# Order of the 512- and 256-column products in each projection chunk, and the pooling product in two sums

## The chip, the cores and the metric

The kernel runs on one core of a Trainium2 chip. The metric is device microseconds of one execution. The kernel before took 885.79 us, the median of three runs (885.66 to 886.0). A run with the profiler on gives the trace from which everything below is read.

## The reference

A two-layer encoder trunk over 256 tokens of 1024 channels in float32. Each layer has a token mixer and a gated MLP, both after an RMSNorm and with a residual:

```
u, q, k, v, g_pool, g_attn = split(norm(h) @ w_in)
pooled   = centred_mean(u[group], window) - u[group]       # 4 groups of 256 channels
pool_out = einsum('bsgc,gcd->bsgd', pooled, w_pool) * pool_scale
attn_out = dilated attention over q, k, v                   # 12 heads in 3 groups
merged   = sigmoid(g_pool) * (pool_out @ w_a) + sigmoid(g_attn) * (attn_out @ w_b)
h = h + merged @ w_o
h = h + (gelu(conv3(a)) * g) @ w_down,   a, g = split(norm(h) @ w_up)
```

After the second layer comes a last RMSNorm.

## The kernel before

**Products in parts.** TensorE multiplies operands of type fp32r. To keep the accuracy, every float32 operand is split in two: a high part (the value cast to fp32r, by ScalarE) and a low part (the value minus the high part, by VectorE). A product is then the sum of three: high by high, low by high, high by low. For a weight this is `wh` and `wl` (lines 177 and 178); for the activations the high and low parts of one channel block lie side by side in the tile `x2` (shape: 8 channel blocks, 2 parts, 256 tokens), so that `x2[:, k]` is 512 columns (both parts) and `x2[:, k, 0]` the 256 columns of the high part.

**A chunk.** `proj` (line 485) makes 128 output channels for all 256 tokens. For each of the 8 blocks of input channels, `two_sums` (line 478) issues two products into one PSUM tile of 512 columns: `wh(k)` over the 512 columns of `x2[:, k]` (line 482), and `wl(k)` over the 256 columns of `x2[:, k, 0]` into the right half of the tile (line 483). The two alternate, so a chunk is eight pairs of a 512-column and a 256-column product. The left half then holds high by high, the right half both mixed sums; ScalarE copies the right half out and VectorE adds the left (`add_up`, lines 503 and 504, or their scaled forms at 970 and 971).

**Where chunks stand.** A layer has 96 chunks: 8 for the pooling input (line 806), 24 for queries and keys (line 954), 8 for the product with `w_a` (line 979), 16 for the gates (line 989) and 40 for the up projection (lines 1072, 1081, 1082). In two layers that is 192. The product with `w_b` (line 1008) calls `two_sums` too, with 4 blocks, in 8 half chunks a layer. Everything else on TensorE (values, scores, residual products at lines 508 to 510, transposes) does not go through it. In the residual products, runs of 512-column products follow one another, and at the end runs of 256-column ones; each has a weight load of its own, as every product here has.

**The pooling branch.** For each of four groups, VectorE forms the window sums and `pd`, and the split of `pd` is kept in two tiles, `plh` for the high and `pll` for the low parts (lines 795, 796, 830 to 834). They take the buffers tagged `ybig` and `xn`. Later `pool_out` (line 835) multiplies them by `w_pool` with `chunk_mm` (line 471): per 128 output channels two blocks of three 256-column products, all into one sum of 256 columns. ScalarE scales this into the high part of `po2` (line 848), VectorE forms the low part (line 849). `pool_out` is a generator: one step of it, two such sums, is placed ahead of each of the four chunks of the second pair of heads (lines 952 to 954).

**Buffers and order.** PSUM has four buffers of 512 columns with the tag `mm`; chunk, gate and pooling sums take them in turn, and a buffer is free once its reader on VectorE is done. Weights come through three raw buffers, loaded by the queue on SyncE, and five split buffers for `wh` and `wl` each; `W.get` has the split of the next three pieces made ahead. The order of the instructions on each engine is fixed when the program is built.

Of the kernel before, what the change touches and what calls it, by code (L numbers as in the profile page):

```python
# [10 lines left out]
F32 = mybir.dt.float32  # L11
F32R = mybir.dt.float32r
AF = mybir.ActivationFunctionType
ALU = mybir.AluOpType
AX = mybir.AxisListType

P = 128
D = 1024
S = 256
DEPTH = 2  # L20
KD = D // P
# [183 lines left out]
def encoder(ctx, tc, x, w_in, w_pool, pool_scale, w_a, w_b, w_o, norm1, norm2, w_up, conv_w,  # L205
            conv_b, w_down, rel_bias, norm_f, onehot, edges, out):
    nc = tc.nc
    const = ctx.enter_context(tc.tile_pool(name="const", bufs=1))
    wpool = ctx.enter_context(tc.tile_pool(name="weights", bufs=1))
    big = ctx.enter_context(tc.tile_pool(name="big", bufs=1))  # L210
    sm = ctx.enter_context(tc.tile_pool(name="small", bufs=2))
    acc = ctx.enter_context(tc.tile_pool(name="acc", bufs=4, space=bass.MemoryType.PSUM))
    mmp = ctx.enter_context(tc.tile_pool(name="mmp", bufs=4, space=bass.MemoryType.PSUM))
# [21 lines left out]
    for l in range(DEPTH):  # L235
        for g in range(NG):
            c0 = C_V + g * 512
            slots = (("m2", 0, 2), ("m2", 1, 2), ("ybig",), ("at2",)) if g == 0 else ()
            for j in range(2):
                tag = "k1" if l == 0 and g == 1 and j == 0 else None  # L240
# [227 lines left out]
        nc.sync.dma_start(out=ov[:, t, 512:], in_=xn[:, 512:])  # L468
        yield

    def chunk_mm(ps, wh, wl, xh, xl, nk):

        for k in range(nk):
            nc.tensor.matmul(ps, wh(k), xh[:, k], start=(k == 0), stop=False)
            nc.tensor.matmul(ps, wh(k), xl[:, k], start=False, stop=False)
            nc.tensor.matmul(ps, wl(k), xh[:, k], start=False, stop=(k == nk - 1))

    def two_sums(ps, wh, wl, x2, nk):


        for k in range(nk):
            nc.tensor.matmul(ps, wh(k), x2[:, k], start=(k == 0), stop=False)  # L482
            nc.tensor.matmul(ps[:, 1], wl(k), x2[:, k, 0], start=False, stop=(k == nk - 1))  # L483

    def proj(x2):

        i, (wh, wl) = W.get()
        ps = mmp.tile([P, 2, S], F32, tag="mm", name="proj_ps")
        two_sums(ps, lambda k: wh[:, k, :], lambda k: wl[:, k, :], x2, KD)
        W.free(i)  # L490
        return ps[:, 0], ps[:, 1]

    def halves(a):

        return a.rearrange("p (t m) -> p t m", t=2)

    def in_order(a):

        return a.rearrange("p (m t) -> p t m", t=2)

    def add_up(out, sums):

        nc.scalar.copy(out=out, in_=sums[1])
        nc.vector.tensor_add(out=out, in0=sums[0], in1=out)  # L504
# [65 lines left out]
    def v_tile():  # L570
        return acc.tile([P, 512], F32, tag="acc", name="v_ps")
# [11 lines left out]
    def two_parts(tag, name):  # L583


        return big.tile([P, KD, 2, 2, P], F32R, tag=tag, name=name)
# [161 lines left out]
    for l in range(DEPTH):  # L748
# [25 lines left out]
        else:  # L774
            for g in range(NG):
                held = begun[0] if g == 0 else [W.get() for _ in range(4)]
                for t in range(2):
                    if g + t == 0:
                        ps = begun[1]
                    else:  # L780
                        ps = v_tile()
# [10 lines left out]
        g2 = gain(norm2[l])  # L792


        plh = big.tile([P, KD, 2, P], F32R, tag="ybig", name="plh")
        pll = big.tile([P, KD, 2, P], F32R, tag="xn", name="pll")
        pooled = {}
        for gi in range(3, -1, -1):
            w = WINDOWS[gi]
            u = sm.tile([P, 2, S + 2 * PAD], F32, tag="u", name="u")  # L800
            nc.vector.memset(u[:, :, 0:PAD], 0.0)
            nc.vector.memset(u[:, :, PAD + S :], 0.0)
            for j in range(2):
                if l == 0:
                    next(bias, None)
                add_up(in_order(u[:, j, PAD : PAD + S]), [halves(a) for a in proj(x2)])
            cur, n = u, S + 2 * PAD
            sh = 1
            while sh < w:
                nxt = sm.tile([P, 2, S + 2 * PAD], F32, tag="us", name="us")  # L810
                n -= sh
                nc.vector.tensor_add(
                    out=nxt[:, :, 0:n], in0=cur[:, :, 0:n], in1=cur[:, :, sh : sh + n]
                )
                cur = nxt
                sh *= 2
            hw = w // 2
            o = PAD - hw
            e = edge[:, gi, 0:hw].unsqueeze(1).to_broadcast([P, 2, hw])
            nc.vector.tensor_mul(out=cur[:, :, o : o + hw], in0=cur[:, :, o : o + hw], in1=e)  # L820
            if hw > 1:
                e = edge[:, gi, hw : w - 1].unsqueeze(1).to_broadcast([P, 2, hw - 1])
                r = slice(o + S - hw + 1, o + S)
                nc.vector.tensor_mul(out=cur[:, :, r], in0=cur[:, :, r], in1=e)
            pd = sm.tile([P, 2, S], F32, tag="us", name="pd")
            nc.vector.scalar_tensor_tensor(
                out=pd, in0=cur[:, :, o : o + S], scalar=1.0 / w, in1=u[:, :, PAD : PAD + S],
                op0=ALU.mult, op1=ALU.subtract,
            )
            ph, pl = plh[:, 2 * gi : 2 * gi + 2], pll[:, 2 * gi : 2 * gi + 2]  # L830
            pd = pd.rearrange("p k (m t) -> p k t m", t=2)
            nc.scalar.copy(out=ph, in_=pd)
            nc.vector.tensor_sub(out=pl, in0=pd, in1=ph.bitcast(F32))
            pooled[gi] = (ph, pl)
        def pool_out(po2):
            for j in range(2):
                i, (wh, wl) = W.get()
                for gg in range(2):
                    ph, pl = pooled[2 * j + gg]
                    for oc in range(2):  # L840
                        ps = mmp.tile([P, 2, P], F32, tag="mm", name="pool_ps")
                        cc = slice(oc * P, (oc + 1) * P)
                        chunk_mm(
                            ps, lambda k: wh[:, 2 * gg + k, cc], lambda k: wl[:, 2 * gg + k, cc], ph, pl, 2
                        )
                        c = 4 * j + 2 * gg + oc
                        sc = hps[:, l, c : c + 1]
                        nc.scalar.activation(po2[:, c, 0], ps, AF.Copy, scale=sc)
                        nc.vector.scalar_tensor_tensor(
                            out=po2[:, c, 1], in0=ps, scalar=sc, in1=po2[:, c, 0].bitcast(F32),  # L850
                            op0=ALU.mult, op1=ALU.subtract,
                        )
                    if gg:
                        W.free(i)
                    yield
# [87 lines left out]
        for m, c in enumerate(PAIRS):  # L943
            if m == 1:
                po2 = two_parts("m2", "po2")
                pool_parts = pool_out(po2)
# [4 lines left out]
            for n in range(4):  # L951
# [4 lines left out]
                scale = HD**-0.5 if n < 2 else 1.0  # L956
                if hd < HPG:
# [3 lines left out]
                        out=lo[:, hd], in0=src, scalar=scale, in1=hi[:, hd].bitcast(F32),  # L961
                        op0=ALU.mult, op1=ALU.subtract,
                    )
                    nc.vector.scalar_tensor_tensor(
                        out=lo[:, hd], in0=rest, scalar=scale, in1=lo[:, hd].bitcast(F32),
                        op0=ALU.mult, op1=ALU.add,
                    )
                else:
# [3 lines left out]
                        out=o, in0=src, scalar=scale, in1=o, op0=ALU.mult, op1=ALU.add  # L972
# [20 lines left out]
        for c in range(KD):  # L993
            th = gate(c)
            nc.vector.scalar_tensor_tensor(
                out=pa[:, c, :], in0=th, scalar=1.0, in1=pa[:, c, :], op0=ALU.add, op1=ALU.mult
# [3 lines left out]
        for c4 in range(2):  # L1000
            ths = [gate(4 * c4 + j) for j in range(4)]
            for j2 in range(2):
                i, (wh, wl) = W.get()
                for j in range(2):
                    c = 4 * c4 + 2 * j2 + j
                    ps = mmp.tile([P, 2, S], F32, tag="mm", name="b_ps")
                    cc = slice(j * P, (j + 1) * P)
                    two_sums(ps, lambda k: wh[:, k, cc], lambda k: wl[:, k, cc], at2, 4)
                    m = sm.tile([P, S], F32, tag="u", name="m")
                    add_up(m, (ps[:, 0], ps[:, 1]))  # L1010
                    nc.vector.scalar_tensor_tensor(
                        out=m, in0=ths[2 * j2 + j], scalar=1.0, in1=m, op0=ALU.add, op1=ALU.mult
                    )
                    nc.vector.tensor_add(out=m, in0=m, in1=pa[:, c, :])
                    m = halves(m)
                    nc.scalar.copy(out=mh[:, c], in_=m)
                    nc.vector.tensor_sub(out=ml[:, c], in0=m, in1=mh[:, c].bitcast(F32))
                W.free(i)
# [43 lines left out]
        held, ps = entry  # L1062
        first = keep_entry(ps)
        ps = v_tile()
# [106 lines left out]
```

## Time and profile before

| | |
|---|---|
| median of three runs | 885.79 us |
| the profiled execution | 885.33 us |
| its span in the trace | 883.5 us |
| TensorE busy | 875.9 us |
| weight loads busy | 755.9 us |
| VectorE busy | 676.8 us |
| ScalarE busy | 520.2 us |
| granted TensorE clock, mean | 0.998 |
| chunk products, 512 columns | 1408 + 128 |
| chunk products, 256 columns | 1408 + 128 |
| half-chunk products (`w_b`), of each width | 64 |
| pooling products, 256 columns | 96 |

The duration that the profile gives for a product (398 ns on average for 512 columns) is the time from its start to its modelled end. Products overlap: the next one starts before the last one's end. What a product costs the stream is therefore the distance from its start to the next start, and this is read from the timeline, where starts are printed to 10 ns. Over a stretch of many products the first and the last start give the pace exactly enough.

### The profile page before, as it was taken

How to read it: one execution, taken by the hardware profiler on the slowest of the kernel's cores; microseconds unless marked ns; L12 is line 12 of the kernel's file. 1: busy time of each engine (PE TensorE's matmuls, PEld its weight loads, DVE VectorE, ACT ScalarE, POOL GpSimd, SP SyncE). 2: the span in 40 equal slices, each digit the busy share in tenths (PEclk: the TensorE clock that was granted, in tenths of full speed). 3: DMA queues.
4: the chain of work that ended last, by engine and by line, in shares of the span. 5: the costliest groups of instructions: out<-in, count | busy, mean ns of one | idle time of the engine just before them, and what ended most of it. 6: DMA issues, size and time to landing. Idle time of an engine off the chain costs nothing.

```text
span 883.5 us, 12773 instructions
## 1 busy us (share of the span) xinstructions
PE 875.9 (99%) x4849; PEld 755.9 (86%) x4849; DVE 676.8 (77%) x1151; ACT 520.2 (59%) x913; POOL 13.1 (1%) x40
## 2 busy tenths in 40 slices
PE   9999999999999999999999999999999999999997
PEld 7889889888888888888888898889888888888886
DVE  6988785767869977877855977766778698787784
ACT  7745554556647756666645564554566477666663
POOL 1000000000000000000000000000000000000000
PEclk9999999999999999999999999999999999999999
DMA  9669744455555475465736555444556447455541
GB/s 332 230 205 307 239 145 144 143 179 188 185 187 191 146 236 190 154 227 191 239 119 213 168 191 191 143 152 134 191 191 218 156 154 231 172 198 187 187 144 48
DMA packets 125790, 164.47 MB, mean 186 GB/s; under 512 B 2995, under 2 KB 106107, under 8 KB 125600
## 3 DMA queue, kind: packets, MB, share of 16 engines
q1 hardware_dynamic: 125712, 163.65, 55.7%
q8 instruction: 38, 0.62, 0.3%
q14 instruction: 24, 0.20, 0.1%
q10 hardware_dynamic: 16, 0.00, 0.0%
HBM read 162.57 MB, written 3.69 MB: 188 GB/s over the span
## 4 chain that ended last, share of the span: by engine, by line
PE 99%; ACT 0%; POOL 0%; DVE 0%; issue 0%; POOLq 0%; ACTq 0%
PE proj_ps L482 41%; PE proj_ps L483 20%; PE res_ps L508 6%; PE res_ps L510 6%; PE v_ps L578 6%; PE res_ps L509 6%; PE v_ps L740 2%; PE b_ps L482 2%; PE v_ps L653 1%; PE pt_ps L903 1%; PE b_ps L483 1%; PE o_ps L924 1%; PE s_ps L874 1%; PE s_ps L869 1%; PE o_ps L920 1%; PE xt_ps L450 1%
## 5 line engine op out<-in xcount | busy, mean ns | idle before, releaser
L482 PE MATMUL proj_ps<-x,wh 128*128 128x512 f32 x1408 | 498.5, 398 | 0.0
L178 DVE TENSOR_TENSOR wl<-raw,wh 128x1024 fp32r<-128x1024 f32 x274 | 334.4, 1223 | 123.5 <-ACT wh L177 121.3
L177 ACT CAST wh<-raw 128x1024 fp32r<-128x1024 f32 x274 | 286.6, 1051 | 189.4 <-PE proj_ps L482 146.2
L483 PE MATMUL proj_ps<-x,wl 128*128 128x256 f32 x1408 | 394.1, 280 | 0.0
L482 PEld LDWEIGHTS proj_ps<-x,wh 128*128 128x128 f32 x1408 | 264.5, 188 | 63.6 <-issue 0.7
L483 PEld LDWEIGHTS proj_ps<-x,wl 128*128 128x128 f32 x1408 | 265.6, 189 | 0.9 <-issue 0.2
L508 PE MATMUL res_ps<-wh,actq 128*128 128x512 f32 (+1 forms) x184 | 70.5, 383 | 0.0
L510 PE MATMUL res_ps<-wh,actk 128*128 128x512 f32 (+1 forms) x184 | 70.1, 381 | 0.0
L509 PE MATMUL res_ps<-wl,actq 128*128 128x512 f32 (+1 forms) x184 | 70.0, 380 | 0.0
L482 PE MATMUL proj_ps<-po,wh 128*128 128x512 f32 x128 | 46.2, 402 | 0.0
L510 PEld LDWEIGHTS res_ps<-wh,actk 128*128 128x128 f32 x184 | 34.6, 188 | 7.0
L508 PEld LDWEIGHTS res_ps<-wh,actq 128*128 128x128 f32 x184 | 34.6, 188 | 6.9
L509 PEld LDWEIGHTS res_ps<-wl,actq 128*128 128x128 f32 x184 | 34.6, 188 | 6.2
L483 PE MATMUL proj_ps<-po,wl 128*128 128x256 f32 x128 | 35.7, 279 | 0.0
L1084 ACT ACTIVATE y<-a,prm 128x256 f32<-128x256 f32 x36 | 21.6, 599 | 18.9 <-DVE a L504 18.8
L1101 ACT ACTIVATE y<-y 128x256 f32<-128x256 f32 x44 | 18.3, 416 | 21.3 <-DVE y L1098 21.3
L482 PEld LDWEIGHTS proj_ps<-po,wh 128*128 128x128 f32 x128 | 24.0, 188 | 5.0
L416 ACT ACTIVATE junk<-h 128x512 f32<-128x512 f32 (+1 forms) x20 | 10.9, 547 | 27.7 <-DVE h L414 27.7
L508 PE MATMUL res_ps<-wh,m 128*128 128x512 f32 (+1 forms) x72 | 26.5, 368 | 0.0
L510 PE MATMUL res_ps<-wh,m 128*128 128x512 f32 (+1 forms) x72 | 26.3, 366 | 0.0
L509 PE MATMUL res_ps<-wl,m 128*128 128x512 f32 (+1 forms) x72 | 26.3, 365 | 0.0
L578 PE MATMUL v_ps<-wh,x 128*128 128x512 f32 x80 | 25.7, 392 | 0.0
(208 smaller groups left out, 1129.6 us busy)
## 6 DMA issues: line engine op xcount, KB each, us to landing
raw<-in_w_in_dram SPq DMA_DIRECT2D x58, 1024.0 KB, 5.4
raw<-in_w_up_dram SPq DMA_DIRECT2D x44, 1024.0 KB, 5.1
raw<-in_w_down_dram SPq DMA_DIRECT2D x22, 1024.0 KB, 4.9
raw<-in_w_a_dram SPq DMA_DIRECT2D x8, 1024.0 KB, 4.9
raw<-in_w_o_dram SPq DMA_DIRECT2D x8, 1024.0 KB, 4.9
raw<-in_w_b_dram SPq DMA_DIRECT2D x4, 1024.0 KB
sk<-fd SPq DMA_DIRECT2D x1, 2560.0 KB
raw<-in_w_pool_dram SPq DMA_DIRECT2D x2, 1024.0 KB
```

Of the source, the lines that this page charges most:

```text
L177: lambda: nc.scalar.copy(out=h, in_=src),
L178: lambda: nc.vector.tensor_sub(out=l, in0=src, in1=h.bitcast(F32)),
L416: nc.scalar.activation(junk[:, 0 : cc.stop - cc.start], h[:, t, cc], AF.Square, scale=D**-0.5, accum_out=ss[:, n : n + 1],)
L482: nc.tensor.matmul(ps, wh(k), x2[:, k], start=(k == 0), stop=False)
L483: nc.tensor.matmul(ps[:, 1], wl(k), x2[:, k, 0], start=False, stop=(k == nk - 1))
L508: nc.tensor.matmul(ps, ah, wh, start=first, stop=False)
L509: nc.tensor.matmul(ps, ah, wl, start=False, stop=False)
L510: nc.tensor.matmul(ps, al, wh, start=False, stop=last)
L578: nc.tensor.matmul(ps, x2[:, 2 * n + j, part, t, :], w[:, j, :], start=(n + m == 0), stop=(n == 3 and m == 5),)
L740: nc.tensor.matmul(ps[t], a[:, k, t, :], w[:, j, :], start=(k + m == 0), stop=(k == KD - 1 and m == 2),)
L1084: nc.scalar.activation(y, a, AF.Identity, bias=b, scale=w1)
L1101: nc.scalar.activation(y2, y2, AF.Tanh, scale=c)
```

## The change

`two_sums` issues first all products of 512 columns of a chunk, then all of 256. The pooled values are kept with both parts side by side, groups 0 and 1 in the buffer `ybig`, groups 2 and 3 in `xn`, so that `pool_out` can call `two_sums` (two products of 512 columns and two of 256 in place of six of 256) on a PSUM tile of 512 columns. The sum is then put together in a small tile `po`, from the buffers tagged `u`, and split from there: four operations in place of two for each 128 channels. `chunk_mm` goes.

```diff
     def two_sums(ps, wh, wl, x2, nk):
         for k in range(nk):
             nc.tensor.matmul(ps, wh(k), x2[:, k], start=(k == 0), stop=False)
+        for k in range(nk):
             nc.tensor.matmul(ps[:, 1], wl(k), x2[:, k, 0], start=False, stop=(k == nk - 1))
...
-        plh = big.tile([P, KD, 2, P], F32R, tag="ybig", name="plh")
-        pll = big.tile([P, KD, 2, P], F32R, tag="xn", name="pll")
+        pl2 = [
+            big.tile([P, KD // 2, 2, 2, P], F32R, tag=tag, name="pl2") for tag in ("ybig", "xn")
+        ]
...
-            ph, pl = plh[:, 2 * gi : 2 * gi + 2], pll[:, 2 * gi : 2 * gi + 2]
+            both = pl2[gi // 2][:, gi % 2 * 2 : gi % 2 * 2 + 2]
+            ph, pl = both[:, :, 0], both[:, :, 1]
...
-                        ps = mmp.tile([P, 2, P], F32, tag="mm", name="pool_ps")
+                        ps = mmp.tile([P, 2, S], F32, tag="mm", name="pool_ps")
                         cc = slice(oc * P, (oc + 1) * P)
-                        chunk_mm(
-                            ps, lambda k: wh[:, 2 * gg + k, cc], lambda k: wl[:, 2 * gg + k, cc], ph, pl, 2
+                        two_sums(
+                            ps, lambda k: wh[:, 2 * gg + k, cc], lambda k: wl[:, 2 * gg + k, cc],
+                            pooled[2 * j + gg], 2,
                         )
                         c = 4 * j + 2 * gg + oc
                         sc = hps[:, l, c : c + 1]
-                        nc.scalar.activation(po2[:, c, 0], ps, AF.Copy, scale=sc)
+                        po = sm.tile([P, 2, P], F32, tag="u", name="po")
+                        nc.scalar.mul(out=po, in_=halves(ps[:, 1]), mul=sc)
                         nc.vector.scalar_tensor_tensor(
-                            out=po2[:, c, 1], in0=ps, scalar=sc, in1=po2[:, c, 0].bitcast(F32),
-                            op0=ALU.mult, op1=ALU.subtract,
+                            out=po, in0=halves(ps[:, 0]), scalar=sc, in1=po, op0=ALU.mult, op1=ALU.add
                         )
+                        nc.scalar.copy(out=po2[:, c, 0], in_=po)
+                        nc.vector.tensor_sub(out=po2[:, c, 1], in0=po, in1=po2[:, c, 0].bitcast(F32))
```

More of the change, by code (lines that the diff above doesn't have):

```diff
@@ L469, in store @@
         yield
[L471 to L476, printed above, removed]
     def two_sums(ps, wh, wl, x2, nk):
@@ L833, in encoder @@
             nc.vector.tensor_sub(out=pl, in0=pd, in1=ph.bitcast(F32))
-            pooled[gi] = (ph, pl)
+            pooled[gi] = both
         def pool_out(po2):
@@ L838, in pool_out @@
                 for gg in range(2):
-                    ph, pl = pooled[2 * j + gg]
                     for oc in range(2):
-                        ps = mmp.tile([P, 2, P], F32, tag="mm", name="pool_ps")
+                        ps = mmp.tile([P, 2, S], F32, tag="mm", name="pool_ps")
                         cc = slice(oc * P, (oc + 1) * P)
-                        chunk_mm(
-                            ps, lambda k: wh[:, 2 * gg + k, cc], lambda k: wl[:, 2 * gg + k, cc], ph, pl, 2
+                        two_sums(
+                            ps, lambda k: wh[:, 2 * gg + k, cc], lambda k: wl[:, 2 * gg + k, cc],
+                            pooled[2 * j + gg], 2,
                         )
```

## The prediction, made before the changed kernel ran

> **What bounds the kernel now.** I read the page first: span, busy shares, and the chain that ended last.
>
> ```profile
> span 883.5 us, 12773 instructions
> PE 875.9 (99%) x4849; PEld 755.9 (86%) x4849; DVE 676.8 (77%) x1151; ACT 520.2 (59%) x913; POOL 13.1 (1%) x40
> PE 99%; ACT 0%; POOL 0%; DVE 0%; issue 0%; POOLq 0%; ACTq 0%
> ```
>
> The chain of waits is TensorE from end to end. So the time is the sum of the distances between the starts of products, and only a step that alters these distances counts, or one that makes another engine late enough to stop TensorE. Products overlap, so their own durations are no costs here.
>
> Second, the timeline of TensorE, for the distances. A pair (512 columns, then 256) in the MLP stage, and in the gates stage, first and last start of a stretch of nothing but pairs:
>
> ```profile
> 393.52 0.40 PE L482 MATMUL proj_ps<-x,wh 128*128 128x512 f32 x1
> ...
> 404.12 0.40 PE L482 MATMUL proj_ps<-x,wh 128*128 128x512 f32 x1
> ```
>
> ```profile
> 180.88 0.39 PE L482 MATMUL proj_ps<-x,wh 128*128 128x512 f32 x1
> ...
> 194.75 0.39 PE L482 MATMUL proj_ps<-x,wh 128*128 128x512 f32 x1
> ```
>
> The first is 30 pairs in 10.60 us, 0.3533 a pair; the second 40 pairs in 13.87, 0.3468. The same two instructions thus cost 2% more in one stage than in the other, with the clock at full speed in both. A view of such stretches by window, with TensorE's busy time and the number of products of the chunk tile, tells how the kernel divides:
>
> ```profile
> core 0: us, PE busy (x), PEclk, DMA share, GB/s
> 55.66:77.96 22.30, 22.30 (x128) 1.00 0.86 255
> 92.19:111.98 19.79, 19.79 (x112) 1.00 0.64 213
> 309.21:320.50 11.29, 11.29 (x64) 1.00 0.83 274
> 477.72:511.63 33.91, 33.91 (x192) 1.00 0.58 187
> 612.50:640.20 27.70, 27.70 (x160) 1.00 0.55 184
> ```
>
> Half the count is pairs: 0.348, 0.353, 0.353, 0.353 and 0.346 a pair. The DMA share does not follow the pace (0.86 in a cheap stretch, 0.58 in a dear one), so it is not the loads. I take the 80 chunks of the MLP by the row at 309.21 as dear, with the 12 at 477.72 and the 7 at 92.19; the 32 of the gates by the row at 612.50 as cheap, with the 8 at 55.66; the rest, between heads, as half and half. That is about 70 to 30: a chunk of eight pairs takes 8 x 0.3533 = 2.827 or 8 x 0.3468 = 2.774, 2.81 us on average.
>
> **The order in a chunk: 192 chunks.** It removes and adds no product; it turns eight pairs into a run of eight 512s and a run of eight 256s. Each needs its own price. A long run of 512s, well under way:
>
> ```profile
> 21.14 0.39 PE L740 MATMUL v_ps<-wh,xul 128*128 128x512 f32 x1
> ...
> 32.02 0.39 PE L740 MATMUL v_ps<-wh,xul 128*128 128x512 f32 x1
> ```
>
> 48 products in 10.88 us, 0.227 each. That would be 1.82 for eight. But a run does not begin at this pace when 256s stood before it. Three places of the trace show a run of 512s that follows a 256, each with its first and its ninth start:
>
> ```profile
> 303.76 0.40 PE L508 MATMUL res_ps<-wh,actq 128*128 128x512 f32 x1
> ...
> 305.58 0.39 PE L510 MATMUL res_ps<-wh,actk 128*128 128x512 f32 x1
> ```
>
> ```profile
> 234.27 0.39 PE L508 MATMUL res_ps<-wh,m 128*128 128x512 f32 x1
> ...
> 236.11 0.39 PE L510 MATMUL res_ps<-wh,m 128*128 128x512 f32 x1
> ```
>
> ```profile
> 320.50 0.40 PE L508 MATMUL res_ps<-wh,actq 128*128 128x512 f32 x1
> ...
> 322.37 0.40 PE L510 MATMUL res_ps<-wh,actk 128*128 128x512 f32 x1
> ```
>
> Eight cost 1.82, 1.84 and 1.87. In the last one that is 0.234 each, the price of the steady run not reached within a chunk's length. None of the three follows a run of 256s, only pairs, so for the new chunk I take the middle between the ends, 1.85, and keep both.
>
> A run of 256s after a run of 512s, first and ninth start, and one after pairs, the twelve of a pooling step up to the next chunk:
>
> ```profile
> 253.34 0.28 PE L508 MATMUL res_ps<-wh,m 128*128 128x256 f32 x1
> ...
> 254.29 0.28 PE L510 MATMUL res_ps<-wh,m 128*128 128x256 f32 x1
> ```
>
> ```profile
> 82.22 0.28 PE L474 MATMUL pool_ps<-plh,wh 128*128 128x256 f32 x1
> ...
> 83.66 0.40 PE L482 MATMUL proj_ps<-x,wh 128*128 128x512 f32 x1
> ```
>
> Eight cost 0.95 in the first; twelve cost 1.44 in the second, eight of them 0.96. The new chunk is 1.85 + 0.955 = 2.805 us, with ends 1.82 + 0.95 = 2.77 and 1.87 + 0.96 = 2.83, against 2.81: 192 x -0.005 = -1.0 us, with ends -7.7 and +3.8. The gain of a steady run is about eaten by the change of width, which a chunk now makes twice and hardly recovers from.
>
> The Trainium skill says under "TensorE: Matmul & The Clock Gate", in "Step-by-step: what each phase is for", that the weight load has an SBUF read port of its own and takes nothing from a running product; and in "Back-to-back issue gap" that the gap is the columns over 2.4 GHz plus 2.5 ns. An estimate by that page is 216 and 109 ns, 2.60 us a chunk in any order, so no gain at all from this step. The trace has 2.77 to 2.83, and two prices for one pair, so it disagrees, and the sum above goes by the rows.
>
> **The half chunks of `w_b`: 16.** They stand among the gates, at the cheap pace: 4 x 0.3468 = 1.387. New: half of what eight cost above, 0.91 to 0.935 for four 512s and 0.475 to 0.48 for four 256s, 1.385 to 1.415; with 1.40, 16 x 0.013 = +0.2 us.
>
> **The pooling product: 8 steps.** A step was the twelve 256s just shown, 1.44 us. It becomes twice (two 512s, two 256s), as many of each as a half chunk, 1.385 to 1.415, with two more changes of width that no row prices; with 1.40, 8 x -0.04 = -0.3 us.
>
> **The pooling sum's extra operations: 16 casts, 16 subtractions.** Nearest rows and the stage in both layers:
>
> ```profile
> L1017 DVE TENSOR_TENSOR m<-m,m 128x256 fp32r<-128x256 f32 x16 | 6.4, 420 | 0.0
> L1016 ACT CAST m<-m 128x256 fp32r<-128x256 f32 x16 | 6.2, 405 | 3.5 <-DVE m L1014 3.5
> 78.00:92.20 14.20, 14.20 (x99) 13.08 (x98) 11.65 (x17) 9.97 (x18) 0.00 (x0) 1.00 0.97 322
> 511.00:526.00 15.00, 15.00 (x102) 13.78 (x101) 9.50 (x15) 8.62 (x16) 0.00 (x0) 1.00 0.76 255
> ```
>
> Per layer VectorE gets 8 x 0.42 = 3.4 us more, ScalarE 8 x 0.41 = 3.2. In layer 0 VectorE has 14.20 - 11.65 = 2.55 free, so it falls behind by up to 0.8; in layer 1 it has 5.5, ScalarE 4.2 and 6.4. What is late next is the release of a PSUM buffer. The tightest one I find: VectorE's reads of the first two pooling sums start at 81.35 and last 0.87, the second set of sums takes the first of these buffers at 82.94, and the next chunk the other at 83.66.
>
> ```profile
> 81.35 0.87 DVE L849 SCALAR_TENSOR_TENSOR po<-pool_ps,hps,po 128x256 fp32r<-128x256 f32 x2
> 82.94 0.28 PE L474 MATMUL pool_ps<-plh,wh 128*128 128x256 f32 x1
> ```
>
> The buffers are free at 81.8 and 82.2, 1.1 and 1.4 us ahead. In the built order both reads still stand ahead of the new subtractions, and later ones are behind by at most 0.8. I cost this at nothing; without that cover it is 0.8 us. The small tile `po` shares two buffers with the pooling input, so ScalarE's scaling of one sum waits for VectorE's subtraction two sums earlier; behind it stand casts of weights, which run up to three pieces ahead.
>
> **Moved, at no cost.** `wh` is now read for the last time eight 256s (0.95 us) before the chunk's end, and `wl` for the first time 1.85 us after its start:
>
> ```profile
> ACT wh L177 <- PE proj_ps L482: 146.2, 127, 2.3
> ```
>
> ScalarE waits 146 us in all for `wh` to be read out, off the chain; it may start earlier, `wl` has more time, and neither can stop TensorE more than before. The raw loads on SyncE's queue keep their order. The new buffers for the pooled values are each written later or freed no later than the old ones.
>
> Sum: -1.0 + 0.2 - 0.3 = -1.1 us on the profiled execution's 885.33 (a span of 883.5 and 1.8 around it), 884.2. The median of the runs, 885.79, stands 0.46 above it, so 884.7.
>
> **Rivals.** *The runs settle at once* (34%). The new chunk begins after eight 256s in step, not after pairs; if that is the better start, eight 512s cost 1.82 to 1.84 as at 303.76 and 234.27, a chunk 2.77 to 2.80. With 2.785: 192 x -0.025 = -4.8, on the median's 885.8, so 881.0; at the end 878.1. For it: two of the three places. Against: at 320.50 eight products were not enough to settle.
>
> *Every chunk pays the dear start* (20%). Each chunk is the case of 320.50, with 256s that cost 0.96: 2.83, 192 x 0.02 = +3.8, 889.6. It decides once the eight 512s take over 1.865. For it: that place stands in the MLP, where 80 of the 192 chunks are; against: the last 256s of a run lie 0.12 apart, as regular as anything in the trace, whereas 320.50 comes out of the uneven pairs.
>
> *VectorE becomes the bound in the pooling stage* (3%). If the 0.8 us reach TensorE in both layers, with the chunk as forecast, +1.6: 886.4; it turns slower only with part of the second rival.
>
> **How the numbers follow.** What a measurement of this kernel can tell from no change I take as 0.2%, 1.8 us. My forecast, the switch of width costs what the pairs' unevenness cost, has 43%, and its own range is 884.0 to 887.5. Faster is the first rival, 34%; slower the second and third, 23%. The range reaches into both, short of the lowest end: 879.5 to 889.6.
>
> **What would show it.** In the changed profile, starts of line 482 from the first to the ninth product of a chunk (1.85 forecast, 1.82 or less and 1.87 or more the rivals), then eight 256s in 0.95 to 0.96; the same length for all chunks, no longer two paces; TensorE's idle column still 0.0 in front of pooling products; a pooling step of 1.40. I am wrong if a chunk lies outside 2.80 to 2.815, or if TensorE waits for VectorE anywhere.

## The result, and the profile after

The changed kernel took 881.65 us, the median of five runs (881.34 to 882.08), beside 885.77 for the kernel before in the same comparison (five runs, 885.02 to 886.0). The ratio is 0.9957, with a 95% interval of 0.9946 to 0.9968: faster by 0.43%, about 4.1 us. The profiled execution took 882.08 us.

The page of the changed kernel, span, busy shares, and the chain that ended last by engine:

```profile
span 880.3 us, 12800 instructions
...
PE 872.4 (99%) x4817; PEld 757.5 (86%) x4817; DVE 682.5 (78%) x1167; ACT 525.6 (60%) x929; POOL 14.0 (2%) x40
...
PE 99%; ACT 0%; POOL 0%; DVE 0%; issue 0%; POOLq 0%; ACTq 0%
```

The chain is TensorE from end to end, as before, and VectorE and ScalarE have become 5.7 and 5.4 us busier. So the gain must lie in the distances between products. The timeline of TensorE gives the first chunk's first product and the last chunk's first product of a run, in the kernel before and then in the changed one:

```profile
41.88 0.48 PE L482 MATMUL proj_ps<-x,wh 128*128 128x512 f32 x1
...
852.22 0.40 PE L482 MATMUL proj_ps<-x,wh 128*128 128x512 f32 x1
```

```profile
42.37 0.48 PE L475 MATMUL proj_ps<-x,wh 128*128 128x512 f32 x1
...
848.73 0.40 PE L475 MATMUL proj_ps<-x,wh 128*128 128x512 f32 x1
```

From the one to the other it is 810.34 us before and 806.36 after, 3.98 less. The first chunk started 0.49 later in this execution, though nothing ahead of it was changed; over the kernels of this study that start lay between 41.7 and 42.4. This stretch, called the *inner time* below, is free of that.

Each product's distance to the next start, summed in the trace by the tile that it writes, divides the 3.98 (us):

```
                                   before    after   difference
chunks                            539.69   536.42     -3.27
half chunks of w_b                 22.19    22.45     +0.27
pooling sums                       11.47    11.15     -0.32
residual products                 143.03   142.60     -0.42
transposes in the attention         6.63     6.33     -0.30
all others                         87.33    87.40     +0.07
```

The stretches of chunks, by window, answer to those shown of before, with the same chunks in each:

```profile
core 0: us, PE busy (x), PEclk, DMA share, GB/s
56.11:78.56 22.45, 22.45 (x128) 1.00 0.85 258
92.52:112.07 19.55, 19.55 (x112) 1.00 0.68 216
309.26:320.41 11.15, 11.15 (x64) 1.00 0.66 217
476.51:510.00 33.49, 33.49 (x192) 1.00 0.59 198
610.13:638.03 27.90, 27.90 (x160) 1.00 0.52 173
```

The window of twelve chunks at 476.51 went from 33.91 to 33.49 us, while the last, with the gates, went from 27.70 to 27.90: the two paces of the kernel before have become one, which lies between them. A chunk, from its first 512 over its first 256 to the next chunk:

```profile
98.10 2.00 PE L475 MATMUL proj_ps<-x,wh 128*128 128x512 f32 x8
99.94 1.11 PE L477 MATMUL proj_ps<-x,wl 128*128 128x256 f32 x8
100.89 0.40 PE L475 MATMUL proj_ps<-x,wh 128*128 128x512 f32 x1
```

The eight 512s take 1.84 us and the eight 256s 0.95. Of the 192 chunks, 134 follow another chunk directly. All of these cost 2.793 to 2.795; before, they cost 2.773 to 2.831, 2.810 on average. A chunk that follows a run of 512s is another case:

```profile
269.85 1.98 PE L475 MATMUL proj_ps<-x,wh 128*128 128x512 f32 x8
271.66 1.12 PE L477 MATMUL proj_ps<-x,wl 128*128 128x256 f32 x8
272.62 0.38 PE L1056 MATMUL a_turn<-ident,a_rows 128*128 128x128 f32 x2
```

Here the 512s take 1.81 us, 0.227 each from the first: 2.77 for the chunk. There are 17 such chunks (14 behind residual products, 3 behind those of the values), and before they cost 2.810. The distances of single products (in ns, from the trace) show where the chunk pays:

```
before, gates:        231 112  233 117  231 113  232 118 ...
before, MLP:          241 120  236 113  233 117  241 120  236 113  233 117 ...
after, behind a 256:  233 236 229 232 231 227 226 227   113 119 120 120 120 120 120 120
after, behind a 512:  226 227 227 226 227 227 226 227   113 119 120 120 120 120 120 120
```

In the settled state a 512 is 227 and a 256 is 120 apart, eight of each 2.774 us. The pairs of the gates alternate at this sum; the pairs of the MLP repeat a pattern of three that costs 53 ns more a chunk; the new order pays 27 ns in the first five 512s and has 8 back in the first two 256s.

### The profile page after: what moved, and what is told of

Read it like the earlier page. It is cut to its first block, busy times and chain, and to the rows that moved or that the text cites. A ratio compares the mean times of both kernels' runs of the same rounds, so it can differ in the third digit from the quotient of the medians.

```text
span 880.3 us, 12800 instructions
## 1 busy us (share of the span) xinstructions
PE 872.4 (99%) x4817; PEld 757.5 (86%) x4817; DVE 682.5 (78%) x1167; ACT 525.6 (60%) x929; POOL 14.0 (2%) x40
## 4 chain that ended last, share of the span: by engine, by line
PE 99%; ACT 0%; POOL 0%; DVE 0%; issue 0%; POOLq 0%; ACTq 0%
PE proj_ps L475 40%; PE proj_ps L477 21%; PE res_ps L502 6%; PE v_ps L572 6%; PE res_ps L503 6%; PE res_ps L504 6%; PE v_ps L734 2%; PE b_ps L475 2%; PE v_ps L647 1%; PE b_ps L477 1%; PE pool_ps L475 1%; PE o_ps L922 1%; PE s_ps L872 1%; PE pt_ps L901 1%; PE s_ps L867 1%; PE o_ps L918 1%
## 5 line engine op out<-in xcount | busy, mean ns | idle before, releaser
L475 PE MATMUL proj_ps<-x,wh 128*128 128x512 f32 x1408 | 354.1, 393 | 0.0
L475 PEld LDWEIGHTS proj_ps<-x,wh 128*128 128x128 f32 x1408 | 254.1, 189 | 47.3 <-issue 0.5
L477 PEld LDWEIGHTS proj_ps<-x,wl 128*128 128x128 f32 x1408 | 192.0, 190 | 13.8
L477 PE MATMUL proj_ps<-x,wl 128*128 128x256 f32 x1408 | 196.3, 282 | 0.0
L475 PE MATMUL proj_ps<-po,wh 128*128 128x512 f32 x128 | 33.1, 400 | 0.0
L1083 DVE SCALAR_TENSOR_TENSOR y<-a,prm,y 128x255 f32<-128x255 f32 x36 | 17.3, 480 | 8.1 <-ACT y L1082 8.1
```

Of the source, the lines that this page charges most:

```text
L1083: nc.vector.scalar_tensor_tensor(out=y[:, 1:], in0=a[:, : S - 1], scalar=w0, in1=y[:, 1:], op0=ALU.mult, op1=ALU.add)
```

## The experiments

**One half of the change at a time.** First the order in `two_sums` alone, with the pooling branch as in the kernel before:

```diff
         for k in range(nk):
             nc.tensor.matmul(ps, wh(k), x2[:, k], start=(k == 0), stop=False)
+        for k in range(nk):
             nc.tensor.matmul(ps[:, 1], wl(k), x2[:, k, 0], start=False, stop=(k == nk - 1))
```

> The order of the products alone; the pooling branch as before the change. Theory A (the price of a product depends on the widths that stand before it, and the chunks gave the gain): chunks of 2.793 us as in the changed kernel, pooling steps of 1.44 as before, so 881.65 + 8 x 0.045 = 882.0 us. Rival B (the pooling branch gave most of it): 885 or more. Rival C (the later need of wl gave it, by ending waits that the profile does not show): 882.0 too, but then the second product of the first pair, not the run, is where a chunk got shorter.

Then the pooling branch alone: the changed kernel with this one line taken out again.

> The pooling branch in two sums, with its products and those of all chunks alternating as before the change. Theory A: a pooling step is four pairs of 0.347 to 0.353 us, 1.39 to 1.41 in place of 1.44, and nothing else: 885.77 - 8 x 0.04 = 885.4 us. Rival B: 882.5 or less.

Measured: the order alone 882.01 us (881.83 to 882.32), ratio 0.9956 [0.9943, 0.9968]; the pooling branch alone 884.95 (884.35 to 886.92), ratio 0.9997 [0.9988, 1.0006], that is, no change. The inner times are 806.73 and 810.01, so 3.61 and 0.33 less than before, and these add up to 3.94 of the 3.98. With the order alone the chunks cost 2.793 again; with the pooling branch alone they keep their two paces, 2.810 on average. The gain is that of the order. That `wl` is needed later, the other explanation set down for the order, is not what brings it: groups of two and pairs in the gates, both below, need `wl` earlier again, and their chunks cost 2.787 and 2.774, less than the 2.793 of eight and eight.

**Other lengths of the runs.** If the price comes from each change of width, shorter runs must cost more; if it comes from a pattern of distances that each order settles into, it need not. Groups of two, and of four:

```diff
+GROUP = 2
...
-        for k in range(nk):
-            nc.tensor.matmul(ps, wh(k), x2[:, k], start=(k == 0), stop=False)
-        for k in range(nk):
-            nc.tensor.matmul(ps[:, 1], wl(k), x2[:, k, 0], start=False, stop=(k == nk - 1))
+        for k0 in range(0, nk, GROUP):
+            for k in range(k0, min(k0 + GROUP, nk)):
+                nc.tensor.matmul(ps, wh(k), x2[:, k], start=(k == 0), stop=False)
+            for k in range(k0, min(k0 + GROUP, nk)):
+                nc.tensor.matmul(ps[:, 1], wl(k), x2[:, k, 0], start=False, stop=(k == nk - 1))
```

> The changed kernel, with each chunk in four groups of two 512s and two 256s. Theory A: as the pooling step of the changed kernel, which is such groups, 1.394 us for four products of each width, so 2.788 a chunk against 2.793: 881.65 - 192 x 0.005 - 16 x 0.009 = 880.5 us. Rival D (each change of width costs, the longer the run the better): four times the changes of the changed kernel, 884 us or more, nearer to the pairs than groups of four are.

> The changed kernel, with each chunk in two groups of four 512s and four 256s. Theory A: as two half chunks of w_b in the changed kernel, 1.401 + 1.406 = 2.807 us a chunk: 881.65 + 192 x 0.014 = 884.3 us, slower than groups of two. Rival D: between groups of two and the changed kernel, faster than groups of two.

Groups of two: 880.47 us (879.85 to 880.66), ratio 0.9936 [0.9924, 0.9948]. Groups of four: 884.54 (883.72 to 885.47), ratio 0.9986 [0.9978, 0.9995]. The timeline of groups of two, the first products of two chunks in a row, and the same for groups of four:

```profile
186.19 0.63 PE L477 MATMUL proj_ps<-x,wh 128*128 128x512 f32 x2
...
188.98 0.62 PE L477 MATMUL proj_ps<-x,wh 128*128 128x512 f32 x2
```

```profile
187.31 1.09 PE L477 MATMUL proj_ps<-x,wh 128*128 128x512 f32 x4
...
190.11 1.09 PE L477 MATMUL proj_ps<-x,wh 128*128 128x512 f32 x4
```

The chunk costs 2.787 us (distances 233 231 113 119, then 233 236 116 112) against 2.807. With eight changes of width groups of two are cheaper than the new kernel with two changes, and groups of four, with four changes, are dearer than both. The number of changes does not set the price.

**Pairs where pairs are cheap.** The gates and the half chunks of `w_b` have got dearer by the change, 2.774 to 2.793 and 1.387 to 1.4035. Here they alternate again, and all other chunks stay as in the changed kernel. The switch is set to 1 ahead of the gates and back ahead of the MLP:

```diff
+        if GROUPS[0] == 1:
+            for k in range(nk):
+                nc.tensor.matmul(ps, wh(k), x2[:, k], start=(k == 0), stop=False)
+                nc.tensor.matmul(ps[:, 1], wl(k), x2[:, k, 0], start=False, stop=(k == nk - 1))
+            return
```

> The changed kernel, but with alternating pairs in the 32 chunks of the gates and the 16 half chunks of w_b; runs everywhere else. Theory A (what stands before decides the pace of the pairs, and here 128-column products stand before, as they did before the change): pairs at 0.3468, a chunk 2.774 in place of 2.793 and a half chunk 1.387 in place of 1.4035: 881.65 - 32 x 0.019 - 16 x 0.0165 = 880.8 us. Rival E (the pace belongs to the stage or drifts, and nothing in the order fixes it): pairs at 0.353 as in most stages, 881.65 + 32 x 0.034 + 16 x 0.01 = 882.9 us.

Measured: 880.59 us (880.52 to 881.03), ratio 0.9944 [0.9931, 0.9958]. Ten gate chunks, first and last start:

```profile
180.91 0.39 PE L477 MATMUL proj_ps<-x,wh 128*128 128x512 f32 x1
...
208.65 0.39 PE L477 MATMUL proj_ps<-x,wh 128*128 128x512 f32 x1
```

That is 2.774 a chunk: the price by place adds up. The pairs are cheap here although chunks of runs, not of pairs, stand in the stages ahead; what stands directly ahead in both kernels are the 128-column products of the attention. This run alone doesn't tell the stage from what stands ahead, since the gates were cheap before too. The kernel with the pooling branch alone does, at one place: in the pooling stage of layer 0 the first two chunks behind a pooling step cost 2.773 there, where the step consists of pairs, and 2.832 in the kernel before, where it is a run of 256s.

**Runs of sixteen.** Two chunks at a time: the 512s of both, then the 256s of both, for 168 of the 192 chunks. It needs two weights split and two PSUM buffers at once.

```diff
+        for ps, (_, (wh, _)) in zip(sums, got):
+            for k in range(KD):
+                nc.tensor.matmul(ps, wh[:, k, :], x2[:, k], start=(k == 0), stop=False)
+        for ps, (_, (_, wl)) in zip(sums, got):
+            for k in range(KD):
+                nc.tensor.matmul(ps[:, 1], wl[:, k, :], x2[:, k, 0], start=False, stop=(k == KD - 1))
```

> The changed kernel, with two chunks at a time in 168 of the 192: sixteen 512s, then sixteen 256s. Theory A: the second eight 512s and the second eight 256s cost what a settled run costs, 1.813 and 0.960, so two chunks take 1.841 + 1.813 + 0.952 + 0.960 = 5.566 us, 2.783 a chunk: 881.65 - 168 x 0.010 = 880.0 us. Rival D agrees in sign; its size would be half of what separates groups of four from groups of eight.

Measured: 882.97 us (881.95 to 883.52), ratio 0.9967 [0.9955, 0.9980], 3 us above what was expected. The price of the chunks is not the reason. Two of them, from the timeline:

```profile
185.50 3.82 PE L498 MATMUL proj_ps<-x,wh 128*128 128x512 f32 x16
189.15 2.08 PE L501 MATMUL proj_ps<-x,wl 128*128 128x256 f32 x16
191.06 0.40 PE L498 MATMUL proj_ps<-x,wh 128*128 128x512 f32 x1
```

They cost 5.56 us, 2.78 each, as expected. The view of waits (engine and line that waits, engine that releases it; us in all, times, longest) has rows that the changed kernel does not have:

```profile
PE pool_ps L475 <- DVE q L989: 0.7, 1, 0.7
PE proj_ps L498 <- DVE po L866: 0.6, 1, 0.6
PE proj_ps L498 <- DVE k L989: 0.3, 1, 0.3
```

All three lie between 80 and 90 us, in the pooling stage of layer 0, where VectorE reads the PSUM buffers too late for the next products. The distances there are 568, 946 and 838 ns where 120 is usual, and 336 to 338 behind each where 227 is: 2.3 us more in all, which covers the 1.95 by which the profiled execution (881.95, the lowest of the five) lies above the expectation. The median lies another 1.0 higher, and no trace shows that part. The reason that suggests itself is that two sums are in hand at once. So the same kernel again, with single chunks in the pooling stage:

> Two chunks at a time as in e6, except in the four chunks a layer among which the pooling steps stand. Theory A (e6's chunks cost what was expected, 5.566 us for two, and its loss is TensorE waiting for VectorE to free PSUM buffers in that stage): 881.65 - 160 x 0.010 = 880.0 us, and no product before which TensorE waits. Rival F (VectorE and ScalarE get their sums too late everywhere when two chunks end together): 882 or more, with waits in other stages.

```profile
PE proj_ps L475 <- DVE po L866: 1.1, 1, 1.1
```

Measured: 881.03 us (880.54 to 883.95), ratio 0.9951 [0.9938, 0.9965]. The expectation was 880.0 and no wait; the median lies 1.0 above it, the profiled execution (880.54) 0.5, and a wait of 1.1 us was still there, with single chunks in that stage. Two sums in hand at once are therefore not the whole reason. The chain of waits that ends in this one (start, us, what):

```profile
76.73 0.94 ACT wh L177
77.67 7.51 DMA raw<-in_w_in_dram
...
85.20 1.06 ACT wh L177
...
86.28 1.23 DVE wl L178
87.51 0.33 DVE po L870
87.84 0.41 DVE po L866
...
88.30 0.73 PE proj_ps L475 x2
```

As a cast on ScalarE ends, the load of the next weight piece begins, at 77.67, and takes 7.5 us; VectorE, whose order is fixed, must split that piece before it comes to the pooling sum. VectorE sat idle for 2.11 us ahead of this split. In the changed kernel the load began at 76.69, VectorE's idle time there was 0.45, and no product waited. The last two of the three waits of the run before stand behind the same load (77.90 to 84.90, VectorE idle for 1.23). What comes late in this stage is thus a weight piece, and VectorE passes the delay on.

**What each order settles into.** Three more orders, whose price no earlier run gives. The 256s one step behind the 512s they belong to (so 512 512 256 512 256 and on, 256 256 at the end), and two steps behind:

```diff
+        for k in range(nk + BEHIND):
+            if k < nk:
+                nc.tensor.matmul(ps, wh(k), x2[:, k], start=(k == 0), stop=False)
+            if k >= BEHIND:
+                j = k - BEHIND
+                nc.tensor.matmul(ps[:, 1], wl(j), x2[:, j, 0], start=False, stop=(j == nk - 1))
```

> The changed kernel, but in each chunk the 256s follow their 512s one step behind: two 512s, six pairs of a 256 and a 512, two 256s. Theory A says that such a chunk costs the same wherever chunks follow one another, between 2.773 (pairs at their cheap pace) and 2.830; which of them it does not say. Cheap: 881.65 - 130 x 0.02 = 879.0 or a little less; dear: 885 to 887.

> As e8, with the 256s two steps behind their 512s: three 512s, five pairs, three 256s. Theory A: one price for all chunks that follow one another, between 2.773 and 2.830 us; 879 to 887, not further told.

And a group of two at the start of each chunk, pairs behind it:

```diff
+        cuts = (0, 2, *range(3, nk + 1)) if nk == KD else range(0, nk + 1, 2)
+        for k0, k1 in zip(cuts, cuts[1:]):
```

> The changed kernel, but each chunk begins with a group of two 512s and two 256s and goes on in pairs. Theory A: the pairs' pace is set by what stands before them, here the group of two; if it leaves them at the cheap pace, a chunk is 0.697 + 6 x 0.347 = 2.778 us and the time 881.65 - 192 x 0.015 = 878.8; if at the dear one, 0.697 + 6 x 0.353 = 2.815 and 885.9. The same for all chunks that follow one another.

One behind: 885.40 us (885.02 to 885.91), ratio 0.9997 [0.9988, 1.0006], chunks of 2.818 and 2.822, near the dear end of the pairs in nearly all places. Two behind: 883.45 (883.08 to 884.34), ratio 0.9974 [0.9964, 0.9984]; here the chunks did not have the one price that was expected, but 2.787, 2.813 and 2.806 in a cycle of three. Two and then pairs: 882.38 (881.81 to 886.14), ratio 0.9965 [0.9955, 0.9975]. The first product of four chunks in a row of that kernel:

```profile
184.46 0.63 PE L477 MATMUL proj_ps<-x,wh 128*128 128x512 f32 x2
...
187.28 0.63 PE L477 MATMUL proj_ps<-x,wh 128*128 128x512 f32 x2
...
190.05 0.62 PE L477 MATMUL proj_ps<-x,wh 128*128 128x512 f32 x2
...
192.87 0.63 PE L477 MATMUL proj_ps<-x,wh 128*128 128x512 f32 x2
```

2.82, 2.77 and 2.82 us: chunks of the same instructions in the same order take a dear and a cheap price in turn, both of which were set down as possible, but as one price for all. What a chunk costs thus depends on the state in which the chunk before left TensorE, not on its own order alone. This kernel also has a wait of 0.2 us, in front of the chunk at 88.03, and the chain behind it is like the one shown for two chunks at a time, with the load of a weight piece from 77.97, 6.95 us long. It has no two chunks in hand anywhere.

**The two best together.** Groups of two, and pairs in the gates and in the half chunks of `w_b`, by the same switch as above.

> The two best orders put together: groups of two 512-column and two 256-column products everywhere, but alternating pairs in the 32 gate chunks and the 16 half chunks of w_b. Theory A (the price of a chunk is set by the order inside it and by what stands before it, and prices of different places add up): the gates' chunks cost 2.773 to 2.774 us in place of 2.787, the half chunks 1.387 in place of 1.394, all other chunks 2.787 as with groups of two everywhere, so 880.5 - 32 x 0.013 - 16 x 0.007 = 879.9 us. Theory F (the gates' low price with pairs depends on the run of 256s that stood before the stage and is not reached after groups of two): the gates' chunks cost 2.82 to 2.83 there, 880.5 + 32 x 0.04 = 881.8 us.

Measured: 879.30 us (878.98 to 879.82), ratio 0.9928 [0.9915, 0.9942]; the gates' chunks cost 2.773 and 2.774, the others that follow a chunk 2.785 to 2.790. It is faster than the kernel before and lies below all runs of the changed kernel. That it is better than groups of two everywhere isn't shown: the inner time is 0.36 us shorter (804.56 against 804.92), but the two intervals overlap.

All prices of a chunk behind its like (us), and what they are above the settled 2.774:

```
pairs, cheap                     2.773     0
groups of two                    2.787   +13 ns
two chunks at a time             2.783    +9
eight and eight (the change)     2.793   +19
two then pairs, mean             2.796   +22
two behind, mean                 2.801   +27
groups of four                   2.807   +33
one behind                       2.820   +46
pairs, dear                      2.827   +53
```

## Why the prediction was right or wrong

**What bounds the kernel** held: the chain is TensorE alone, and the time followed the sum of distances. Past the kernel's first microseconds, the exceptions among the runs are the three with waits in the pooling stage (both kernels with two chunks at a time, and two then pairs), where the chain runs back over a weight load.

**The old chunk**, 2.81 us from the split of 70 to 30, was right: the 134 chunks that follow a chunk, those behind residual products and those behind the values all average 2.810. (The counts in the working, 99 chunks dear, 40 cheap and 53 half and half, are 65 to 35; 91 of the 134 were dear, 68%. All of these give 2.81.) The view of the two prices was right too. What they go with, which the prediction left open, is what stands ahead: behind the attention's 128-column score and output products the pairs were nearly always cheap, behind transposes, residual products and pooling sums dear, chunk after chunk until the next such place. It is no strict rule: after score products at 561 us the pairs were dear (2.830).

**The new chunk** is the step that failed, in its size. "None of the three follows a run of 256s, only pairs, so for the new chunk I take the middle between the ends, 1.85": eight 512s behind a run of 256s took 1.841, and the 256s 0.952, so 2.793 in place of 2.805. On 134 chunks that is -1.6 us. The second of the three rows, 234.27, had the right value, and the first rival came nearest: it had the run begin better behind a run of 256s than at 320.50. But the run doesn't settle at once, as that rival has it; it settles with the sixth product. That the even distances of the 256s are the reason is not shown: behind pairs in their dear pattern eight 512s cost 1.87 at fourteen places, but 1.82, less than here, at two. The rival's price of 2.785 was 8 ns too low, and its 881.0 us lies 0.65 below the median. The median lies outside the 884.0 to 887.5 that the forecast had for its likeliest case, and the condition set for it, a chunk between 2.80 and 2.815, did not hold. It lies within the range of 879.5 to 889.6 because that range reached into both rivals: what came is close to the branch with 34%, not the forecast with 43%.

**The sum took all chunks alike**, and that was the second part of the miss: "the same length for all chunks" holds behind chunks, half chunks and pooling sums alone. Behind residual products and values the 512s of the new order lie at the settled distance from the first, 2.77 a chunk in place of 2.81, -0.7 us on 17 chunks. And the runs of residual products, which the change doesn't touch, start more cheaply behind a run of 256s than behind pairs. The first and the ninth start of the one that the prediction showed at 303.76:

```profile
303.80 0.40 PE L502 MATMUL res_ps<-wh,actq 128*128 128x512 f32 x1
...
305.64 0.39 PE L504 MATMUL res_ps<-wh,actk 128*128 128x512 f32 x1
```

Eight cost 1.84 here and at all sixteen such places behind a chunk; before, fourteen of these cost 1.87 and two, the one at 303.76 and its like in layer 1, 1.82. That is -0.32 of the -0.42 in the table of distances. The transposes' -0.30 was not in the sum either. The four together, -1.6, -0.7, -0.4 and -0.3, make up the 3.0 us between the forecast's -1.1 and the measured -4.1.

**Half chunks and pooling steps** came as forecast. Four half chunks, first start to the start behind them, and one pooling step:

```profile
212.29 1.09 PE L475 MATMUL b_ps<-at,wh 128*128 128x512 f32 x4
...
217.91 0.40 PE L475 MATMUL proj_ps<-x,wh 128*128 128x512 f32 x1
```

```profile
78.56 0.63 PE L475 MATMUL pool_ps<-pl,wh 128*128 128x512 f32 x2
79.03 0.39 PE L477 MATMUL pool_ps<-pl,wl 128*128 128x256 f32 x2
...
79.96 2.00 PE L475 MATMUL proj_ps<-x,wh 128*128 128x512 f32 x8
```

A half chunk is 1.40 (1.40 forecast), a step 1.40 (1.40 forecast; 1.394 to the ns): +0.27 and -0.32 us for +0.2 and -0.3.

**The cover for the extra operations of the pooling sum** held. The pooling stage by window in both layers (columns: TensorE, weight loads, VectorE, ScalarE, GpSimd), the waits of TensorE, and the read of the first two sums with the product that takes a buffer next:

```profile
78.20:92.52 14.32, 14.32 (x86) 12.61 (x85) 13.31 (x23) 11.94 (x24) 0.00 (x0) 1.00 0.94 319
509.64:523.96 14.32, 14.32 (x86) 12.60 (x85) 11.53 (x20) 11.45 (x23) 0.00 (x0) 1.00 0.79 271
```

```profile
PE gain_ps L333 <- DVE ones L319: 1.0, 1, 1.0
PE v_ps L647 <- ACT xuh L603: 0.2, 1, 0.2
```

```profile
81.48 0.87 DVE L846 SCALAR_TENSOR_TENSOR po<-pool_ps,hps,po 128x256 f32<-128x256 f32 x2
...
82.75 0.63 PE L475 MATMUL pool_ps<-pl,wh 128*128 128x512 f32 x2
```

TensorE is busy for all of the 14.32 us in both layers, and its only two waits are those at the start, which the kernel before has too. VectorE has 1.0 us left in layer 0 where it had 2.55, and the two sums are read by 82.35, 0.4 ahead of the next one. The cover is thin: in the three kernels in which the weight piece of this stage came 1 us later, it was gone, and TensorE waited behind it for 0.2 to 1.2 us. The working looked for what the extra operations take from VectorE, not for how long VectorE itself waits for weights. The rival "VectorE becomes the bound" did not come (its 886.4, 884.7 and 1.6, should read 886.3), nor did "every chunk pays the dear start": the eight 512s stayed under its 1.865.

**The moved reads of `wh` and `wl`** cost nothing that can be seen. By the two waits above no product waits for a weight in the chunks, and ScalarE still waits for products:

```profile
ACT wh L177 <- PE proj_ps L475: 128.4, 106, 3.1
```

Weight loads of the first chunks, between 46 and 57 us, wait for a cast or a split three times, 0.24 us each, where before it was once; the four chunks there cost 11.88 us in all, beside 11.86 before.

**The estimate of 2.60 us.** By the formula of the Trainium skill, "TensorE: Matmul & The Clock Gate", section "Back-to-back issue gap", the chunk would be 2.60 us in any order, as an estimate. The prediction left out that the Trainium skill gives this formula there for a single product by itself, and about 131 ns a product of 512 columns for a stream in which every product has its weight load. Neither is what the trace has: a settled 512 is 227 ns from the next, and behind another chunk a chunk is 2.77 to 2.83, by the order. So the measurement decides here, as the prediction had it.

## What to carry to other kernels

Where the chain is TensorE alone, read the price of products from the distances of their starts, for each order and each predecessor, before a reorder is costed: the same products differ here by up to 2% by order, and a change of order also re-prices what follows it. Don't expect fewer changes of width to be better; try groups of two, and leave each stage the order that is cheap there. A reorder that holds two PSUM buffers at once, or moves the moment at which a weight load can begin, needs the margin of the buffers' readers checked first.

## What the runs showed of the hardware that was not expected

- One and the same pair of products has two lasting prices, 346.7 ns (distances 231 to 233 and 112 to 118) and 353.3 (a pattern of three pairs, 241 120 236 113 233 117), and keeps the one it fell into for whole stages. The dear pattern came back to the ns in both layers.
- The price does not grow or fall steadily with the length of the runs: 2.787, 2.807, 2.793 and 2.783 us a chunk for groups of two, four, eight and sixteen.
- The state passes from chunk to chunk: two prices in turn with a group of two ahead of pairs, a cycle of three with the 256s two steps behind.
- A run of 512s behind even 256s is dearer in its first five products (229 to 236 against 227), and the first 256s behind 512s are cheaper (113 and 119 against 120).

What makes the distances so is open. The runs show which order has which price, with the granted clock at full speed in the stages compared and no wait in them; none of them looks into the machine that spaces the products.
